# One-hot gates one tile later, and v rows ahead of u rows while the queries run

## The chip, the core and the metric

The kernel runs on one core of a Trainium2 chip. The metric is device time in microseconds (us) from start to end of one execution; the median of several executions is compared. The core has five engines with their own instruction streams: TensorE (PE, matmuls, with its weight loads shown as PEld), VectorE (DVE), ScalarE (ACT), GpSimd (POOL) and SyncE (SP). Here POOL issues the indirect gathers and SP issues nearly all other transfers.

## The reference, cut to what matters

One layer of a decoder: a state-space branch and a dilated attention branch are merged, and then each of 1,088 tokens goes through a retrieval layer (PEER) with 16,384 single-neuron experts. The change lies in this last layer. For a block of tokens it computes:

```
q = xb @ w_qp                                   # 8 heads, 2 halves of 128
s = q . sub_keys                                # 8 x 2 x 128 scores per token
sv, si = top_k(s, 16)                           # per head and half
cand = sv[0][:, None] + sv[1][None, :]          # 256 sums per head
best, pos = top_k(cand, 16); eidx = cidx[pos]   # 128 experts per token
gate = softmax(best)
act = gelu(xb . u_tab[eidx])                    # 128 dot products per token
out = (gate * act) . v_tab[eidx]                # 128 weighted rows per token
```

## The kernel before

The tokens are worked in two halves. The **first half** (512 tokens, four tiles of 128) gathers the rows of its chosen experts. The **second half** (512 tokens and 64 sample tokens, five tiles, the last of 64) computes all 16,384 experts densely. The gathers of the first half run beside the second half's work.

**The gather** (`gather`) is a Python generator that emits one row at a time. A *u row* (`gather_u`, L1558) is one indirect DMA on POOL of 128 expert rows of 1,024 floats (one per token) into one of eight `row` buffers (`RB`), followed by a multiply with row sum on DVE (L1562, "dot"). A *v row* of tiles 0 and 1 (`gather_v`, L1624) brings the 128 experts of one token; four of them make a batch that PE sums on column strips (L1640), with one small copy on DVE (L1635). The v rows of tiles 2 and 3 (`gather_w`, L1590) are added on DVE (L1596) and wait for the dense stage. So each tile has 128 u rows and 128 v rows. Which comes next is decided by

```python
pick = int(made[0] - made[1] >= LEAD)   # LEAD = 160; 1 is a v row
if not can[pick]:
    pick = 1 - pick
```

so that v rows start once u rows are 160 ahead and the two then take turns. How many rows are emitted is set by `tick(us)`: the surrounding code calls it with an estimate of its own time, and each row uses up 1.9 of it, times a rate that `pace` sets for the stage. `after` pins each row's instructions behind the last matmul (or, in `choose`, the last reduction) emitted before them. The dots and strip matmuls are emitted some rows later than their DMA (`late`, `catch_up`).

**The second half's routing** is `peer_keys(1)`, in this order: the norm of five tiles; the *queries*, 16 columns `c`, each a product with `w_qp` (L80, copied out by ACT at L1266), the scores against 128 keys (into a `tr` bank of PSUM, of which there are two) and `top16` of five tiles on DVE (L1304 to L1308, 25 instructions a column); then for each tile `choose` (DVE only: candidate sums L1330, eight `top16`, and 16 instructions that find the expert numbers, L1353 and L1354) and `gates`. `gates` turns a tile's choices into the dense gate matrix: DVE makes one-hots of the expert's row and column number for four tokens at a time (L1392, tile `oij`), ACT scales one by the gate (L1395, four instructions), PE multiplies them, ACT copies the result (L1397) into `Gt`, and after 32 tokens (a *block*; 18 blocks in all) `Gt` goes to DRAM (`G_scr`).

Between these steps `early` computes a block of 128 dense scores ahead (48 matmuls into `tr`, gelu on ACT at L1408, the weight split on ACT at L134 and DVE at L136): six times in each `choose`, once after each block of `gates`, twice in the queries; 50 in all. Then the dense stage begins, and its first weights read a piece of every block of `G_scr`.

The order of instructions on an engine is not wholly the order of the code: a list scheduler takes, at each free moment of an engine in its own estimate of time, the earliest instruction in code order that is ready. On the chip each engine then works through its list in that fixed order.

Of the kernel before, what the change touches and what calls it, by code (L numbers as in the profile page):

```python
# [36 lines left out]
FILL = (1.1, 2.274, 0.0, 0.8, 1.5, 0.05)  # L37
RATES = (1.0, 1.3, 1.0, 1.0, 0.86, 1.0, 0.6)
RB = 8
GL = 20  # L40
GO = (2, 0, 0.7)
LEAD = 160

VT = (2, 3)
SSMT = (10.0, 0.0, 5.0)
# [22 lines left out]
class Prog:  # L68
    def __init__(self, tc, a, stop=None):
        self.tc, self.nc, self.a, self.stop = tc, tc.nc, a, stop  # L70
        self.marks = []
        self.sides, self.inside, self.last, self.dn = {}, False, None, None

    def mark(self, name):
        n = [i.name for i in self.nc.cur_bb.bb.instructions[-1:]]
# [7 lines left out]

        self.sides[name] = [gen, rate, 0.0]

    def pace(self, name, rate):
        if name in self.sides:
            self.sides[name][1] = rate

    def tick(self, us):  # L90
        if self.inside:
            return
        for name in list(self.sides):
            s = self.sides[name]
            s[2] += us * s[1]
            while s[2] > 0 and name in self.sides:
                c = self.step(name)
                if name == "ahead":
                    us += c
# [1132 lines left out]
    def peer_keys(self, h):  # L1232
        tc, nc, a = self.tc, self.nc, self.a
        v = nc.vector
        nt = NT[h]
        ntl = len(TILES[NT[h]])
        es2 = ExitStack()
        self.pace(*(("gather", RATES[6]) if h else ("ahead", FILL[1])))
        x, (xp, g, x2) = self.xf, self.x2sb
        with ExitStack() as es:  # L1240
            esj = ExitStack()
            jk = esj.enter_context(tc.tile_pool(name=f"jk{h}", bufs=1, side="left" if h else "right"))
            for i in range(ntl):
                rows = 128 if i < 4 else 64
                r0 = h * 512 + i * 128 if i < 4 else 1024
                xn = jk.tile([128, D], F32, name="xn", tag="xn", bufs=2 + h)[128 - rows:]
                self.rms(xp, x2[i][128 - rows:], g[128 - rows:], xn, xn)
                if h == 0:
                    nc.sync.dma_start(self.xn2[r0:r0 + rows], xn)
                self.to_t(xn, rows, x, i * 128, 128 - rows)  # L1250
                self.tick(4.0)
            esj.close()
            self.esx2.close()
            if h:
                da = es.enter_context(tc.tile_pool(name="da", bufs=1))
            with tc.tile_pool(name=f"pk{h}", bufs=1, side="right") as kp, ExitStack() as eg:
                self.pace(*(("gather", RATES[2]) if h else ("ahead", FILL[2])))
                sv = [kp.tile([128, 16, 16], F32, name=f"sv{i}") for i in range(ntl)]
                si = [kp.tile([128, 16, 16], U32, name=f"si{i}") for i in range(ntl)]
                kq = eg.enter_context(tc.tile_pool(name=f"kq{h}", bufs=1, side="right"))  # L1260
                for c in range(16):
                    qp = kq.tile([128, nt], F32, name="qp", tag="qp", bufs=2)
                    keys = kq.tile([128, 128], F32, name="keys", tag="keys", bufs=3)
                    nc.sync.dma_start(keys, a["keys"][:, c])
                    for ps, (c0, c1) in zip(self.gemm_f(a["w_qp"][c], x, SPLITS[NT[h]]), SPLITS[NT[h]]):
                        nc.scalar.copy(qp[:, c0:c1], ps[:, :c1 - c0])  # L1266
                    pvs = []
                    for i in range(ntl):
                        rows = 128 if i < 4 else 64
                        if i % 4 == 0:  # L1270
                            ps = self.trt()
                        pvs.append(ps[:rows, (i % 4) * 128:(i % 4) * 128 + 128])
                        self.mm(pvs[i], qp[:, i * 128:i * 128 + rows], keys, start=True, stop=True)
                    for i in range(ntl):
                        rows = 128 if i < 4 else 64
                        rest = kq.tile([128, 128], F32, name="rest", tag="rest", bufs=3)[:rows]
                        self.top16(sv[i][:rows, c], si[i][:rows, c], pvs[i], rest)
                    self.tick(6.0)
                    if h and c in CE:
                        self.early(da, x)  # L1280
                self.pace(*(("gather", RATES[3]) if h else ("ahead", FILL[3])))
                eg.close()
                if h:
                    kg = eg.enter_context(tc.tile_pool(name="kg", bufs=1, side="right"))
                for i in range(ntl):
                    rows = 128 if i < 4 else 64
                    self.choose(kp, h, i, rows, sv[i], si[i], (lambda: self.early(da, x)) if h else None)
                    if h == 0:
                        self.tick(30.0)
                    if h == 0 and i == GO[0]:  # L1290
                        self.beside("gather", self.gather(), GO[1])
                    if h:
                        self.gates(kg, i, rows, lambda: self.early(da, x))
            if h:
                self.mark("dense")
                self.pace("gather", RATES[4])
                dn = self.dn = es2.enter_context(tc.tile_pool(name="dn", bufs=1, side="right"))
                self.dense(dn, da, x)
                es2.close()
        self.espx.close()  # L1300
# [205 lines left out]
    def gather(self):  # L1506
        nc, gp = self.nc, self.gp

        self.strips = gp.tile([128, NS, 2, 63], F32, name="strips")
        nc.gpsimd.memset(self.strips, 0.0)  # L1510
        yield RATE
        self.gw, self.ei = {}, {}

        self.late, self.wait = [], {}
        us, ws = [self.gather_u(i) for i in range(4)], [(self.gather_w if i in VT else self.gather_v)(i) for i in range(4)]

        nu = nv = 0
        made = [0, 0]
        while nv < 4:
            can = [nu < 4 and nu < nv + 3, nv < nu and (nv not in VT or self.dn is not None)]  # L1520
            if not any(can):
                yield RATE
                continue
            pick = int(made[0] - made[1] >= LEAD)
            if not can[pick]:
                pick = 1 - pick
            made[pick] += 1
            if next((us[nu] if pick == 0 else ws[nv]), None) is None:
                nu, nv = nu + 1 - pick, nv + pick
            else:  # L1530
                self.catch_up(2)
                yield RATE
        while self.late:
            self.late.pop(0)[1]()
# [210 lines left out]
```

## Time and profile before

| | |
|---|---|
| median of 3 runs | 4047.9 us (4040.63 to 4048.96) |
| profiled execution | 4032.86 us |
| its span, first to last instruction | 4031.1 us |
| busy share of PE, PEld, DVE, ACT, POOL | 93%, 84%, 73%, 36%, 36% |
| mean granted TensorE clock | 0.961 |

The busy time of an engine is the time in which at least one of its instructions runs; a share of it over the whole span mixes stages with different limits, so the stages have to be read one by one. The granted clock is 1 at 2.4 GHz and 0.5 at 1.2 GHz.

### The profile page before, as it was taken

The numbers are of one execution on the slowest core, as the hardware profiler recorded it, in microseconds if no ns is written. First come the engines' busy times: TensorE is split into PE (matmuls) and PEld (weight loads), VectorE is DVE, ScalarE is ACT, GpSimd is POOL, SyncE is SP. The second block draws the span as 40 slices with busy tenths as digits, with TensorE's granted clock in tenths as the row PEclk, the third lists the DMA queues.
The fourth block names the chain that finished last, engine by engine and source line by source line (L and its number), as shares of the span: only waits on it lengthen the run. The fifth ranks groups of instructions, "written<-read, shape, count | busy, mean of one in ns | idle before, by whom it ended". The sixth has DMA issues, their size and how long they took to land.

```text
span 4031.1 us, 72558 instructions
## 1 busy us (share of the span) xinstructions
PE 3738.5 (93%) x27907; PEld 3380.1 (84%) x27907; DVE 2943.4 (73%) x6796; ACT 1433.1 (36%) x2756; POOL 1444.1 (36%) x1236
## 2 busy tenths in 40 slices
PE   8889989899989967799979999879999999999997
PEld 8789965589878755597859899769999999999997
DVE  8627233445985767866999977668767999889986
ACT  3232224323234316322216888812222222222222
POOL 1620000000004424445563544433346755545550
PEclk9999989899999978899989999989999999999999
DMA  5574579544369989799897899999989999988993
GB/s 166 158 236 154 194 252 343 181 131 163 99 200 318 321 299 306 264 345 346 300 322 262 294 345 337 339 344 332 329 307 338 362 336 331 323 308 306 324 316 111
DMA packets 448987, 1112.83 MB, mean 276 GB/s; under 512 B 44656, under 2 KB 189424, under 8 KB 443008
## 3 DMA queue, kind: packets, MB, share of 16 engines
q1 hardware_dynamic: 301184, 571.26, 41.8%
q0 software_dynamic: 147456, 536.94, 37.0%
q8 instruction: 219, 3.59, 0.4%
q14 instruction: 128, 1.05, 0.1%
HBM read 991.77 MB, written 124.27 MB: 277 GB/s over the span
## 4 chain that ended last, share of the span: by engine, by line
PE 54%; DVE 6%; DMA 6%; issue 2%; ACT 2%; POOL 0%; SPq 0%; DVEq 0%; ACTq 0%; POOLq 0%
PE mm L80 31%; PE tr L80 20%; PE va L1640 2%; DVE row L1562 2%; DMA row<-in_u_tab,ei 1%; DMA G_scr<-Gt 1%; DMA Q<-Q_scr 1%; DVE wL L136 1%; DMA row<-in_v_tab,eT 1%; DMA V<-v_scr 0%; ACT Gt L1397 0%; DMA kT<-k_scr 0%; ACT sm L936 0%; DVE rest L1306 0%; DMA hs_scr<-Y 0%
## 5 line engine op out<-in xcount | busy, mean ns | idle before, releaser
L1558 POOL DMA_INDIRECT row<-in_u_tab,ei x512 | 664.3, 1297 | 986.7 <-DVE row L1562 451.3
L134 ACT CAST wH<-wraw 128x1024 fp32r<-128x1024 f32 (+1 forms) x476 | 492.3, 1035 | 1245.5 <-PE mm L80 915.5
L136 DVE TENSOR_TENSOR wL<-wraw,wH 128x1024 fp32r<-128x1024 f32 (+1 forms) x476 | 577.7, 1214 | 377.7 <-ACT wH L134 365.0
L1562 DVE SCALAR_TENSOR_TENSOR row<-row,gxn 128x1024 f32<-128x1024 f32 x512 | 616.8, 1217 | 48.4 <-DMA row<-in_u_tab,ei 41.8
L80 PE MATMUL tr<-x2H,wH 128*128 128x288 f32 x2048 | 611.7, 299 | 6.4 <-ACT a L1408 4.6
L80 PE MATMUL tr<-x2L,wH 128*128 128x288 f32 x2048 | 609.3, 297 | 0.0
L80 PE MATMUL tr<-x2H,wL 128*128 128x288 f32 x2048 | 609.1, 297 | 0.0
L80 PE MATMUL mm<-WH,wH 128*128 128x288 f32 (+2 forms) x2048 | 474.0, 295 | 18.6 <-ACT WH L186 18.2
L80 PE MATMUL mm<-WL,wH 128*128 128x288 f32 (+2 forms) x2048 | 473.8, 295 | 0.4 <-DVE WL L187 0.4
L80 PE MATMUL mm<-WH,wL 128*128 128x288 f32 (+2 forms) x2048 | 468.1, 294 | 0.0
L1590 POOL DMA_INDIRECT row<-in_v_tab,ei x256 | 350.9, 1371 | 293.3 <-DVE x3v L1596 240.7
L1624 POOL DMA_INDIRECT row<-in_v_tab,eT x256 | 315.7, 1233 | 386.4 <-DVE row L1562 228.4
L80 PEld LDWEIGHTS tr<-x2H,wH 128*128 128x128 f32 x2048 | 385.1, 188 | 16.3 <-ACT a L1408 7.2
L80 PEld LDWEIGHTS tr<-x2L,wH 128*128 128x128 f32 x2048 | 385.1, 188 | 2.5 <-issue 2.5
L80 PEld LDWEIGHTS tr<-x2H,wL 128*128 128x128 f32 x2048 | 385.0, 188 | 2.5 <-issue 2.5
L80 PEld LDWEIGHTS mm<-WH,wH 128*128 128x128 f32 x2048 | 339.8, 188 | 27.3 <-ACT WH L186 19.9
L80 PEld LDWEIGHTS mm<-WL,wH 128*128 128x128 f32 x2048 | 342.0, 188 | 4.1 <-issue 2.5
L80 PEld LDWEIGHTS mm<-WH,wL 128*128 128x128 f32 x2048 | 339.1, 188 | 1.7 <-issue 1.7
L1596 DVE SCALAR_TENSOR_TENSOR x3v<-row,act,x3v 128x1024 f32<-128x1024 f32 x256 | 327.4, 1279 | 3.0 <-DMA x3v<-x_scr 0.7
L80 PE MATMUL mm<-xnH,wL 128*128 128x288 f32 (+1 forms) x960 | 319.9, 333 | 2.7 <-DVE wL L136 2.7
L80 PE MATMUL mm<-xnH,wH 128*128 128x288 f32 (+1 forms) x960 | 322.3, 336 | 0.0
L80 PE MATMUL mm<-xnL,wH 128*128 128x288 f32 (+1 forms) x960 | 319.2, 332 | 0.0
(392 smaller groups left out, 7760.8 us busy)
## 6 DMA issues: line engine op xcount, KB each, us to landing
wraw<-in_vT SPq DMA_DIRECT2D x132, 512.0 KB
wraw<-in_uT SPq DMA_DIRECT2D x128, 512.0 KB
G_scr<-Gt SPq DMA_DIRECT2D x18, 2048.0 KB
G<-G_scr SPq DMA_DIRECT2D x32, 1152.0 KB
cc<-in_kc SPq DMA_DIRECT2D x48, 512.0 KB
cc<-in_vc SPq DMA_DIRECT2D x48, 512.0 KB
wraw<-in_w_g SPq DMA_DIRECT2D x32, 512.0 KB
wraw<-in_w_qp SPq DMA_DIRECT2D x32, 512.0 KB
```

What stands on the lines that cost most here:

```text
L80: self.last = self.nc.tensor.matmul(out, lhsT=lhsT, rhs=rhs, **kw)
L134: nc.scalar.copy(h, raw)
L136: nc.vector.tensor_sub(l, raw, h.bitcast(F32))
L1558: self.after(nc.gpsimd.indirect_dma_start(out=row, out_offset=None, in_=a["u_tab"], in_offset=bass.IndirectOffsetOnAxis(ap=ei[:, k:k + 1], ...
L1562: self.after(v.scalar_tensor_tensor(row, row, 1.0, xn, op0=ALU.mult, op1=ALU.mult, accum_out=act[:, k:k + 1]))
L1590: self.after(nc.gpsimd.indirect_dma_start(out=row, out_offset=None, in_=a["v_tab"], in_offset=bass.IndirectOffsetOnAxis(ap=ei[:, k:k + 1], ...
L1596: self.after(v.scalar_tensor_tensor(x3, row, self.gw[i][:, k:k + 1], x3, op0=ALU.mult, op1=ALU.add))
L1624: self.after(nc.gpsimd.indirect_dma_start(out=row, out_offset=None, in_=a["v_tab"], in_offset=bass.IndirectOffsetOnAxis(ap=eT[:, tk:tk + 1 ...
L1640: self.after(nc.tensor.matmul(va[0][c:c + 32, :], lhsT=self.strips[:, s, j, 31 - t - s:63 - t - s], rhs=rows[s * 2 + j][:, b * 512:(b + 1) ...
```

## The change

Two things are changed. In the second half's routing, the gates of a tile are emitted after `choose` of the next tile; those of the last tile come at the end. And in the norm and the queries of the second half the gather prefers v rows (`want`), with the condition that the u rows of the tile are all emitted and 12 rows more (`LATE`); while that does not hold, it emits u rows. After the queries `want` is empty again and the old rule holds.

```diff
+LATE = 12
...
-    def pace(self, name, rate):
+    def pace(self, name, rate, want=None):
         if name in self.sides:
             self.sides[name][1] = rate
+            if name == "gather":
+                self.want = want
...
-        self.pace(*(("gather", RATES[6]) if h else ("ahead", FILL[1])))
+        self.pace(*(("gather", RATES[6], "v") if h else ("ahead", FILL[1])))
...
-                self.pace(*(("gather", RATES[2]) if h else ("ahead", FILL[2])))
+                self.pace(*(("gather", RATES[2], "v") if h else ("ahead", FILL[2])))
...
-                    if h:
-                        self.gates(kg, i, rows, lambda: self.early(da, x))
+
+                    if h and i:
+                        self.gates(kg, i - 1, 128, lambda: self.early(da, x))
+                if h:
+                    self.gates(kg, ntl - 1, 64, lambda: self.early(da, x))
...
-            pick = int(made[0] - made[1] >= LEAD)
+            if nu < 4 and self.want == "v":
+
+                can[1] = can[1] and (not can[0] or made[0] >= 128 * nv + 128 + LATE)
+            pick = int(made[0] - made[1] >= LEAD) if self.want is None else int(self.want == "v")
             if not can[pick]:
                 pick = 1 - pick
```

## Rows read from the trace of the kernel before

**Rows 1.** The page: head line and busy line of its first part.
```profile
span 4031.1 us, 72558 instructions
...
PE 3738.5 (93%) x27907; PEld 3380.1 (84%) x27907; DVE 2943.4 (73%) x6796; ACT 1433.1 (36%) x2756; POOL 1444.1 (36%) x1236
```

**Rows 2.** Windows by stage: stretch, its length, busy us (instructions) per engine, clock.
```profile
1906.00:2000.00 94.00, 92.90 (x701) 82.25 (x700) 82.72 (x351) 22.00 (x38) 53.92 (x43) 1.00 0.90 303
2000.00:2104.00 104.00, 77.69 (x480) 56.47 (x480) 95.76 (x442) 12.50 (x21) 66.43 (x54) 0.82 0.89 318
2104.00:2157.00 53.00, 49.97 (x377) 44.59 (x376) 52.53 (x246) 18.59 (x29) 29.77 (x22) 1.00 0.92 327
2157.00:2340.00 183.00, 179.87 (x1399) 169.75 (x1398) 173.27 (x460) 149.40 (x321) 73.36 (x44) 0.98 0.79 270
2340.00:2580.00 240.00, 238.30 (x1893) 221.49 (x1893) 169.58 (x215) 205.74 (x461) 108.39 (x82) 1.00 0.98 341
2580.00:2660.00 80.00, 37.03 (x192) 25.53 (x192) 39.51 (x52) 37.83 (x86) 26.10 (x24) 0.71 0.94 339
2660.00:3985.00 1325.00, 1325.00 (x10017) 1294.54 (x10016) 1126.14 (x1639) 354.13 (x495) 657.02 (x497) 1.00 0.89 318
```

**Rows 3.** Windows of 10 us, the last stretch of the queries.
```profile
2090.00:2100.00 10.00, 5.81 (x26) 2.67 (x26) 9.27 (x46) 0.00 (x0) 5.32 (x5) 0.53 0.96 372
```

**Rows 4.** Waits between 1900 and 2120: who waited for whom, us, times, longest.
```profile
ACT qp L1266 <- PE tr L80: 59.7, 12, 9.9
...
ACT act L1568 <- DVE row L1562: 26.0, 1, 26.0
PEld tr L80 <- DVE rest L1306: 25.7, 8, 6.7
```

**Rows 5.** Windows of L1558 alone, the u rows issued by POOL.
```profile
1200.00:1920.00 720.00, 255.36 (x204) 0.92 0.89 313
1920.00:2105.00 185.00, 58.34 (x45) 0.90 0.90 313
2105.00:2624.00 519.00, 110.51 (x80) 0.98 0.90 314
```

**Rows 6.** Windows of L1624 alone, the strip v rows issued by POOL.
```profile
1200.00:1920.00 720.00, 59.48 (x54) 0.92 0.89 313
1920.00:2105.00 185.00, 55.25 (x46) 0.90 0.90 313
2105.00:2624.00 519.00, 115.31 (x80) 0.98 0.90 314
```

**Rows 7.** Windows of L1562 alone, the dots on DVE (two records each).
```profile
1920.00:2105.00 185.00, 54.67 (x90) 0.90 0.90 313
```

**Rows 8.** Chain that ended last: one batch of strips, and the end of the gates.
```profile
1851.33 1.85 PE va L1640 x16
...
2621.16 28.14 DMA G_scr<-Gt
...
2649.49 5.05 DMA G<-G_scr
```

**Rows 9.** Instruction groups by line: busy us, mean ns of one, idle before.
```profile
L134 ACT CAST wH<-wraw 128x1024 fp32r<-128x1024 f32 (+1 forms) x476 | 492.3, 1035 | 1245.5 <-PE mm L80 915.5 <-PE tr L80 187.0 <-issue 97.5
...
L1395 ACT ACTIVATE oij<-oij,T 128x128 f32<-128x128 f32 x576 | 180.2, 393 | 7.3 <-DVE oij L1392 6.9
...
L80 PE MATMUL mm<-oij 128*128 128x128 f32 x1152 | 172.1, 283 | 13.3 <-ACT oij L1395 13.3
...
L1397 ACT COPY Gt<-mm 128x512 f32<-128x512 f32 x144 | 155.1, 1107 | 57.0 <-PE mm L80 56.2
...
L1408 ACT ACTIVATE a<-tr 128x288 f32<-128x288 f32 x256 | 105.3, 412 | 241.2 <-PE tr L80 238.8 <-DVE row L1562 2.4
```

**Rows 10.** Timeline of DVE around the first one-hot.
```profile
2139.97 0.99 DVE L1304 MAX8 best<-look 128x8 f32<-128x50 f32 x8
...
2156.85 1.23 DVE L1392 TENSOR_TENSOR oij<-i,T 128x1024 f32<-128x1024 f32 x1
```

**Rows 11.** Windows of L1640 alone, the strip matmuls (PE, weight loads).
```profile
2105.00:2624.00 519.00, 43.42 (x320) 8.88 (x320) 0.98 0.90 314
2660.00:3985.00 1325.00, 36.56 (x304) 7.93 (x304) 1.00 0.89 318
```

More of the change, by code (lines that the diff above doesn't have):

```diff
@@ L71, in __init__ @@
         self.marks = []
-        self.sides, self.inside, self.last, self.dn = {}, False, None, None
+        self.sides, self.inside, self.last, self.dn, self.want = {}, False, None, None, None
     def mark(self, name):
```

## The prediction

> **What bounds the kernel now.** I read the page first. PE is busy for 93% of the 4031.1 us span [rows 1], and that share hides where it is not. So the second view is the windows by stage [rows 2]. In the dense stage, 2660 to 3985, PE is busy for all of 1325 us at full clock: every PE us that goes there costs one. In the queries, from 2000 to 2104, PE has 77.69 of 104 us and DVE 95.76: DVE sets the pace. From 2104 to 2340 both are nearly full (PE 229.8 and DVE 225.8 of 236, added from two rows). From 2340 to 2580 PE is full (238.30 of 240) and DVE has 70 us free. From 2580 to 2660 PE is busy for 37.03 of 80 us: the early score blocks have run out, and at the end a 28.14 us store of `Gt` and a 5.05 us load of `G` stand alone on the chain [rows 8].
>
> The third view is the waits of the queries [rows 4]. ACT waits 59.7 us for query matmuls, and PE's weight loads wait 25.7 us for `top16` (L1306), which frees the PSUM bank that the next scores need: the lag of DVE reaches PE. By 2090 to 2100 PE is busy for 5.81 of 10 us and the granted clock is 0.53 [rows 3], mostly the lower level of 1.2 GHz, after PE had stood still in pieces.
>
> The fourth view is the rows themselves. By 1920 POOL has issued 204 u rows and 54 strip v rows; in the queries 45 and 46; between 2105 and 2624 80 and 80 [rows 5, 6].
>
> **The change part by part.** *v rows first.* In the queries 91 rows are emitted, and `tick` does not change that. v rows are now taken until tile 0 has its 128: 128 - 54 = 74. Tile 1 may only start at 128 + 128 + 12 = 268 u rows, which is not reached, so the other 17 are u rows. 28 dots leave the queries and 28 v rows, seven batches, enter. A dot costs DVE 54.67 / 45 = 1.215 us [rows 7], together 34 us; a batch costs PE 1.85 us [rows 8], together 13 us.
>
> That is not a gain of 34 us. PE is full from 1906 to 2000 (92.90 of 94 us [rows 2]), and there the seven batches lengthen it, while DVE gets time that it can't use. The columns without dots cost DVE (82.72 + 95.76 - 54.67) / 16 = 7.7 us each, and the last three columns carry all 17 dots: 3 x 7.7 + 17 x 1.215 = 44 us. The first 13 go at PE's pace. PE did about ten columns in the 94 us, some 9.4 us each with five batches; without them 8.5, with 74 / 16 batches' worth of rows (1.4 a column, 2.6 us) 11.1 us. 1906 + 13 x 11.1 + 44 = 2094, against 2104 now: **-10 us**. Bounds: 0, if PE stands still for rows that have not landed (a batch now needs four of the eight buffers and nothing else runs between); -26, if all the idle time of PE from 2000 to 2104 goes. I take -10, which the two paces give.
>
> *The same rows later.* At the end of the queries there are now 221 u and 128 v rows, 93 apart, so the old rule first emits 67 u rows and then alternates. In the 160 rows up to 2624 that is 114 u and 46 v rows: sums of 335 and 174, where there were 329 and 180. The dense stage therefore finds about what it found, and its 36.56 us of strips [rows 11] stay. Between 2105 and 2624 PE loses 34 v rows, more than eight batches; I count the seven that went into the queries, 13 us, in a stretch where PE is busy for 97% or more until 2580: **-13 us**. Bounds: 0 and -16. DVE gets 28 to 34 dots, 34 to 41 us, and first into a stretch where it is full. What hides them is the 70 us that DVE has free from 2340 to 2580 [rows 2], as `choose` is needed only when its gates' turn comes. Without that cover they would cost 34 us.
>
> On this term a rule of the Trainium skill speaks against the sum: the page "Perfetto Trace Analysis", section "Identifying the Most-Contended Engine", says that matmul busy time is no good measure of how full TensorE is and that the share of weight loading is to be read beside it. That share is 221.49 of 240 from 2340 to 2580. By the rule PE had up to 18 us of room there and the 13 us might be nothing; by the matmul row they count. The sum goes by the matmul row, and the other case is a rival below.
>
> *Gates one tile later.* No instruction is added or removed; the six early blocks of each `choose` keep their place in it. In the code the second tile's `choose` now stands before the first gates. But the scheduler already had it there: its `top16` starts at 2139.97, before the first one-hot at 2156.85 [rows 10]. So at the start the move is worth nothing by itself. At the end it is not neutral. Gates of tile 3 and 4, six blocks, now stand behind all of `choose` with six early blocks among them, where there were twelve. A block costs ACT 8 x (180.2 + 155.1) / 144 = 18.6 us and an early block 1.035 + 2 x 0.412 = 1.9 us, 20.5 together [rows 9]. PE needs 8 x 172.1 / 144 = 9.6 us for the block, 48 x 1325 / 10017 = 6.3 us for the early one [rows 2, 9], and about 43.42 / 18 = 2.4 us of strips [rows 11]: 18.3. ACT becomes the slower one, by 2.2 us a block, 13 us over six. Bounds: 0 (the last blocks before had none left either) and +13; between them I take **+8 us**, nearer the upper, since early blocks that are used up sooner leave more of the end bare.
>
> Nothing new waits on SP or POOL: the same DMAs are issued, and only POOL's order of u and v rows changes. What is late next is the DVE work of `choose`, and the ACT list behind the gelu of tile 1's dots, which stood for 26.0 us [rows 4]: that gelu now falls among the gates.
>
> Sum: -10 - 13 + 8 = -15 us. The profiled execution took 4032.86 us, so 4017.9; the median of the runs is 1.0037 times it, so **4033 us**.
>
> **Rivals.**
> *The whole lag goes* (chance 0.12). PE's idle 26 us before 2104 vanish with the dots, and the clock stays up. -26 - 13 + 8 = -31: 4017. For it: the waits on `top16`. Against it: the 17 dots and the next 67 come at once after.
>
> *The strips were not on the path* (0.16). From 2340 to 2580 the work is held by ACT (205.74 of 240) and the weight loads as much as by matmuls; then the 13 us are not earned: -10 + 8 = -2: 4046. The page named above would read it so.
>
> *Only moved* (0.14). DVE is full from 2000 to 2340 and gets the same dots by its end; the 10 us won in the queries are lost again in `choose`, and the 13 us go to an end as long as before plus the 8 us: -13 + 8 = -5: 4043.
>
> *Gates start late* (0.28, the slower side). Two `choose` with some 32 u rows before the first gates, where DVE took 10 dots from 2104 to 2157: 22 x 1.215 = 27 us later, less the 10 won. ACT is busy for 393 of the 503 us from 2157 to 2660 [rows 2] and PE can't let it catch up. 27 - 10 + 8 = +25: 4073. It decides if the scheduler keeps one-hots behind the second `choose`; against it stands how early it mixed them before [rows 10]. It turns slower once the first one-hot lies more than about 10 us later than 2157.
>
> **How the numbers follow.** My forecast has 0.30, the likeliest case; the rivals have 0.12, 0.16, 0.14 and 0.28. A measurement of this kernel can tell about 0.2%, 8 us. Faster by more: the forecast and the whole lag, 0.42. Within it: the strips and the moved case, 0.30. Slower: 0.28. The range reaches from a little below the best case to the worst, 4014 to 4072, and leaves out less than 0.2 at its ends; the forecast's own, by the bounds of its terms, is 4017 to 4046.
>
> **What would show it.** In the queries: about 74 rows of L1624 and 17 of L1558 between the first and the last column, DVE clearly less than full for the first 13 columns, and the last `top16` near 2094. After them: u rows alone for some 67 rows, DVE full to about 2370, strips near 30 us of PE up to the end of the gates. At the end: the last early block more than two gate blocks before the last one. The first one-hot shows the slower rival: near 2157 or before it I am right, 20 us after it I am wrong. The prediction is also wrong if the split of rows at the start of the dense stage differs by more than a few batches, or if PE waits for v rows by more than 10 us in the queries.

## The result, and the profile after

The changed kernel takes 4068.27 us (median of 5 runs, 4064.05 to 4080.39), the kernel before 4046.97 us (5 runs, 4040.63 to 4048.96). The ratio is 1.0061, 95% interval 1.0043 to 1.0078: slower by 25 us by the ratio (0.0061 x 4047; 21 by the medians), where 4033 us and a gain were forecast. The profiled execution took 4067.84 us.

The windows by stage of the kernel after, with the columns of [rows 2]; the cuts are near the last copy of the queries (2088), the end of the last `top16` (2125), the first one-hot (2211) and the last `Gt` copy (2660):

```profile
1920.00:2088.00 168.00, 163.70 (x1231) 127.10 (x1229) 115.43 (x624) 33.37 (x56) 82.83 (x80) 1.00 0.89 304
2088.00:2125.00 37.00, 8.06 (x38) 7.39 (x39) 35.17 (x140) 0.86 (x3) 29.62 (x19) 0.58 0.84 300
2125.00:2211.00 86.00, 84.70 (x638) 84.46 (x637) 84.26 (x277) 29.57 (x48) 50.07 (x36) 1.00 0.92 342
2211.00:2420.00 209.00, 202.60 (x1573) 195.81 (x1571) 197.52 (x507) 167.92 (x356) 81.40 (x51) 0.99 0.81 283
2420.00:2570.00 150.00, 142.73 (x1115) 131.46 (x1116) 109.74 (x131) 127.92 (x290) 61.87 (x49) 0.99 0.95 334
2570.00:2660.00 90.00, 62.59 (x373) 51.76 (x376) 62.35 (x69) 81.27 (x197) 33.61 (x27) 0.88 0.87 283
2660.00:2700.00 40.00, 14.36 (x74) 9.21 (x67) 17.15 (x28) 4.02 (x6) 13.32 (x15) 0.63 0.99 372
2700.00:4020.00 1320.00, 1319.27 (x9972) 1290.03 (x9971) 1114.75 (x1622) 353.30 (x493) 645.46 (x489) 1.00 0.88 315
```

The dense stage is as full as before. In the queries VectorE has the room that was forecast (115.43 of 168 us). The new thing is the second line: for 37 us PE is busy for 8.06, at a granted clock of 0.58, while VectorE is full (35.17). Windows of single lines show what is in that stretch: first the u rows (L1567), then the strip v rows (L1633), then the dots (L1571, two records each), the counterparts of [rows 5 to 7].

```profile
1920.00:2088.00 168.00, 9.99 (x8) 1.00 0.89 304
2088.00:2125.00 37.00, 29.62 (x19) 0.58 0.84 300
2125.00:2211.00 86.00, 50.07 (x36) 1.00 0.92 342
...
1920.00:2088.00 168.00, 72.84 (x72) 1.00 0.89 304
2088.00:2125.00 37.00, 0.00 (x0) 0.58 0.84 300
2125.00:2211.00 86.00, 0.00 (x0) 1.00 0.92 342
...
1920.00:2088.00 168.00, 3.68 (x6) 1.00 0.89 304
2088.00:2125.00 37.00, 20.49 (x34) 0.58 0.84 300
2125.00:2211.00 86.00, 42.07 (x69) 1.00 0.92 342
```

The split of rows is nearly the one forecast, but not its place: 72 v rows and 8 u rows up to the last query copy, then 19 u rows in 37 us and 36 in the next 86, with no v row between. The waits of the kernel after between 1900 and 2120 say why (compare [rows 4]):

```profile
POOL row L1633 <- PE va L1649: 54.9, 18, 7.1
ACT qp L1269 <- PE mm L81: 37.0, 11, 6.2
...
PE tr L81 <- DVE rest L1312: 18.6, 2, 18.0
...
DVE row L1571 <- DMA row<-in_u_tab,ei: 10.1, 2, 8.3
```

While only v rows are fetched, all eight row buffers come free through PE's strips, and POOL stands 54.9 us for them. In the kernel before, its waits for strips were, by the same view:

```profile
POOL row L1558 <- PE va L1640: 14.0, 9, 2.6
...
POOL row L1624 <- PE va L1640: 5.7, 5, 2.5
```

The u rows behind the v rows in POOL's list come late: the first is issued at 2071.9 us, after the query copies of 15 of the 16 columns. That the buffers are the reason is read from these waits; no run had more of them. Then PE stands 18.0 us at a stretch for a PSUM bank whose `top16` (L1312) is queued on VectorE. The timeline of VectorE in the kernel after shows what it is queued behind:

```profile
2081.50 1.22 DVE L1571 SCALAR_TENSOR_TENSOR row<-row,gxn 128x1024 f32<-128x1024 f32 x1 [8.30 <-DMA row<-in_u_tab,ei]
...
2094.46 0.28 DVE L1310 MAX8 sv<-tr 128x8 f32<-128x128 f32 x1
2094.67 1.20 DVE L1571 SCALAR_TENSOR_TENSOR row<-row,gxn 128x1024 f32<-128x1024 f32 x1
2095.80 0.08 DVE L1571 DVE_READ_ACCUMULATOR row<-row,gxn 128x1 f32 x1
2095.80 1.21 DVE L1571 SCALAR_TENSOR_TENSOR row<-row,gxn 128x1024 f32<-128x1024 f32 x1
...
2098.00 0.27 DVE L1312 MATCH_REPLACE8 rest<-sv,tr 128x128 f32<-128x128 f32 x1
2098.20 1.20 DVE L1571 SCALAR_TENSOR_TENSOR row<-row,gxn 128x1024 f32<-128x1024 f32 x1
```

The first dot waits 8.30 us for its row, with `top16` work behind it on the engine; from then on a dot of 1.2 us stands between every few `top16` instructions of 0.28 us.

**From the queries' end to the first one-hot.** This stretch was 89.5 us in the kernel before (2067.4 to 2156.9) and is 122.9 us after (2088.2 to 2211.1). The groups of VectorE in it, by line, of the kernel before:

```profile
L1562 DVE SCALAR_TENSOR_TENSOR row<-row,gxn 128x1024 f32<-128x1024 f32 x21 | 25.3, 1211 | 4.6 <-DMA row<-in_u_tab,ei 4.3 <-DMA gxn<-xn_scr 0.3
L136 DVE TENSOR_TENSOR wL<-wraw,wH 128x1024 fp32r<-128x1024 f32 x8 | 9.7, 1210 | 0.0
...
L1353 DVE TENSOR_TENSOR df<-look,posf 128x128 int32<-128x128 f32 (+3 forms) x11 | 6.1, 557 | 0.1
```

and of the kernel after:

```profile
L1571 DVE SCALAR_TENSOR_TENSOR row<-row,gxn 128x1024 f32<-128x1024 f32 x52 | 62.4, 1213 | 1.8 <-DMA row<-in_u_tab,ei 1.8
L139 DVE TENSOR_TENSOR wL<-wraw,wH 128x1024 fp32r<-128x1024 f32 x14 | 17.1, 1218 | 1.7 <-ACT wH L137 1.7
...
L1359 DVE TENSOR_TENSOR df<-look,posf 128x128 int32<-128x128 f32 (+3 forms) x8 | 5.1, 633 | 0.0
```

31 dots more are 37.1 us, six weight splits more 7.4 us. `choose` itself is not more: of its `df` instructions, the first step in finding the expert numbers and eight a tile, there are 11 before and 8 after.

**The end of the gates.** The copies into `Gt` that come after the last early gelu, by the timeline of that line, in the kernel before:

```profile
L1397 ACT COPY Gt<-mm x18: 1023/1046/1110, 2579.8 to 2620.1; 128x512 f32<-128x512 f32 x18
```

and after:

```profile
L1403 ACT COPY Gt<-mm x42: 986/1052/1106, 2566.7 to 2656.0; 128x512 f32<-128x512 f32 x42
```

Eight copies are a block of gates, and these blocks are bare: no early score block is left to run beside them. 2.25 bare blocks in 40.6 us have become 5.25 in 89.6 us.

**The sum of it** is in the idle time of PE. I count it from a point early in the second half's queries, 920 us after the first query copy of the first half, to 20 us after the first load of `G`. The row of this window of the kernel before:

```profile
1911.70:2669.50 757.80, 680.65 (x5064) 605.42 (x5063) 618.20 (x1770) 446.23 (x952) 355.45 (x267) 0.94 0.90 316
```

and of the kernel after:

```profile
1913.50:2700.00 786.50, 684.00 (x5071) 612.27 (x5072) 624.16 (x1778) 446.14 (x954) 355.72 (x276) 0.94 0.89 310
```

PE is busy for nearly the same (680.65 and 684.00 us) and idle for 77.1 and 102.5: 25.4 of the 28.7 us by which the window is longer. From the first load of `G` to the end of the span it is 1381.6 and 1386.1 us.

Three rows of each kernel show where PE is idle after the last query copy: up to the first one-hot, from there to the last early gelu, and in the bare end. Before:

```profile
2067.40:2156.90 89.50, 73.78 (x507) 58.39 (x508) 83.96 (x393) 22.00 (x35) 53.61 (x42) 0.89 0.91 324
2156.90:2579.50 422.60, 417.77 (x3286) 390.84 (x3286) 342.57 (x673) 354.64 (x779) 181.84 (x126) 0.99 0.89 310
2579.50:2620.10 40.60, 27.28 (x157) 21.93 (x159) 28.93 (x33) 34.63 (x83) 12.61 (x10) 0.87 0.97 346
```

and after:

```profile
2088.20:2211.10 122.90, 92.85 (x675) 91.95 (x676) 119.33 (x416) 30.23 (x50) 79.60 (x55) 0.88 0.90 330
2211.10:2566.40 355.30, 344.11 (x2682) 326.07 (x2680) 303.90 (x634) 292.24 (x636) 143.09 (x99) 1.00 0.87 303
2566.40:2656.00 89.60, 62.55 (x368) 52.50 (x368) 64.38 (x71) 83.82 (x205) 32.79 (x26) 0.87 0.87 283
```

The idle time grows by about 14 us in the first stretch and 14 in the bare end, with 6 between them. So the stretch with the 37 us that catch the eye holds less than half of the growth.

### The profile page after: what moved, and what is told of

The parts are those of the page before. It is cut to its first block, busy times and chain, and to the rows that moved or that the text cites. A ratio compares the mean times of both kernels' runs of the same rounds, so it can differ in the third digit from the quotient of the medians.

```text
span 4066.1 us, 72466 instructions
## 1 busy us (share of the span) xinstructions
PE 3745.3 (92%) x27907; PEld 3391.0 (83%) x27907; DVE 2944.5 (72%) x6796; ACT 1432.6 (35%) x2756; POOL 1432.8 (35%) x1236
## 4 chain that ended last, share of the span: by engine, by line
PE 53%; DVE 5%; DMA 4%; ACT 4%; issue 3%; POOL 1%; SPq 0%; another core or an unknown queue 0%; POOLq 0%; DVEq 0%; ACTq 0%
PE mm L81 31%; PE tr L81 19%; PE va L1649 2%; DVE row L1571 2%; ACT Gt L1403 1%; ACT oij L1401 1%; DMA row<-in_u_tab,ei 1%; DMA row<-in_v_tab,eT 1%; DMA Q<-Q_scr 1%; DMA G_scr<-Gt 1%; ACT sm L939 1%; DVE wL L139 0%; POOL row L1633 0%; ACT wH L137 0%; PE tr L957 0%
## 5 line engine op out<-in xcount | busy, mean ns | idle before, releaser
L1567 POOL DMA_INDIRECT row<-in_u_tab,ei x512 | 669.6, 1308 | 1057.0 <-DVE row L1571 556.6
L1571 DVE SCALAR_TENSOR_TENSOR row<-row,gxn 128x1024 f32<-128x1024 f32 x512 | 617.5, 1220 | 54.7 <-DMA row<-in_u_tab,ei 47.1
L1633 POOL DMA_INDIRECT row<-in_v_tab,eT x256 | 299.3, 1169 | 351.3 <-DVE row L1571 176.4
L81 PEld LDWEIGHTS mm<-WH,wH 128*128 128x128 f32 x2048 | 340.4, 188 | 25.1 <-ACT WH L189 15.9
```

Of the source, the lines that this page charges most:

```text
L81: self.last = self.nc.tensor.matmul(out, lhsT=lhsT, rhs=rhs, **kw)
L1567: self.after(nc.gpsimd.indirect_dma_start(out=row, out_offset=None, in_=a["u_tab"], in_offset=bass.IndirectOffsetOnAxis(ap=ei[:, k:k + 1], ...
L1571: self.after(v.scalar_tensor_tensor(row, row, 1.0, xn, op0=ALU.mult, op1=ALU.mult, accum_out=act[:, k:k + 1]))
L1633: self.after(nc.gpsimd.indirect_dma_start(out=row, out_offset=None, in_=a["v_tab"], in_offset=bass.IndirectOffsetOnAxis(ap=eT[:, tk:tk + 1 ...
```

## The experiments

Each ratio below is to the kernel before on the same chip; its medians there were 4040.87, 4039.25 and 4040.11 us. Prices in us below are the ratio less 1, times 4040. The other columns come from one profiled execution each: from the last query copy to the first one-hot, PE's idle time in the window just defined, and the bare stretch from the last early gelu to the start of the last `Gt` copy.

| kernel | median us | ratio (95%) | to one-hot | PE idle | bare end |
|---|---|---|---|---|---|
| before | | | 89.5 | 77.1 | 40.6 |
| the change | 4068.27 | 1.0061 (1.0043 to 1.0078) | 122.9 | 102.5 | 89.6 |
| gates later alone | 4072.05 | 1.0075 (1.0056 to 1.0094) | 136.8 | 94.6 | 73.7 |
| v first alone | 4075.05 | 1.0082 (1.0064 to 1.0099) | 92.9 | 103.6 | 53.9 |
| change, short dots | 4023.45 | 0.9959 (0.9947 to 0.9971) | 100.7 | 63.9 | 71.4 |
| before, short dots | 4003.52 | 0.9920 (0.9902 to 0.9937) | 82.1 | 56.4 | 24.6 |
| change, early blocks late | 4061.89 | 1.0060 (1.0041 to 1.0079) | 109.7 | 99.2 | 71.1 |
| two v rows, one u row | 4045.43 | 1.0022 (1.0010 to 1.0033) | 89.3 | 78.3 | 49.0 |
| first gates at once | 4054.15 | 1.0044 (1.0026 to 1.0061) | 94.7 | 89.2 | 73.6 |
| the same, early spread | 4046.37 | 1.0022 (1.0008 to 1.0037) | 91.0 | 84.0 | 28.7 |
| all mends | 4038.47 | 1.0001 (0.9988 to 1.0014) | 89.1 | 73.8 | 36.3 |
| before, early spread | 4040.12 | 1.0003 (0.9991 to 1.0014) | 89.9 | 80.9 | 25.1 |
| before, v rows in `choose` | 4033.67 | 0.9987 (0.9972 to 1.0002) | 91.8 | 74.2 | 22.2 |
| the same, more of them | 4058.14 | 1.0045 (1.0028 to 1.0062) | 96.8 | 77.1 | 23.5 |

### The two parts alone

Gates one tile later, the gather as before:

```diff
-                    if h:
-                        self.gates(kg, i, rows, lambda: self.early(da, x))
+                    if h and i:
+                        self.gates(kg, i - 1, 128, lambda: self.early(da, x))
+                if h:
+                    self.gates(kg, ntl - 1, 64, lambda: self.early(da, x))
```

> The move of the gates alone; rows are chosen as before. Theory R (rows): the loss comes from the v rows, which leave the u rows to heap up at the end of the queries (in the changed kernel PE is busy for 10 of the 40 us from 2080 to 2120, and some 20 dots follow each other on VectorE there). Then this kernel is within 8 us of before, with its first one-hot between 2150 and 2175. Theory G (gates): the loss comes from the order of the second choose before the first gates and from the early blocks that are missing among the last six blocks. Then this kernel is 15 to 25 us slower, with its first one-hot at 2190 or later.

The v preference, the gates as before:

```diff
-        self.pace(*(("gather", RATES[6]) if h else ("ahead", FILL[1])))
+        self.pace(*(("gather", RATES[6], "v") if h else ("ahead", FILL[1])))
...
-            pick = int(made[0] - made[1] >= LEAD)
+            pick = int(made[0] - made[1] >= LEAD) if self.want is None else int(self.want == "v")
```

> The preference for v rows alone; each tile's gates follow its own choose as before. Theory R: 15 to 30 us slower than before, the last query product at about 2088 instead of 2067 and PE idle for some 30 us after it. Theory G: within 8 us of before, since the dots that come late are hidden in the gates' time.

Each alone costs about as much as, or more than, both together: 30 and 33 us, where the change costs 25; the intervals leave open whether more. In the first, VectorE's groups between the last query copy and the first one-hot are:

```profile
L1564 DVE SCALAR_TENSOR_TENSOR row<-row,gxn 128x1024 f32<-128x1024 f32 x29 | 34.9, 1214 | 3.3 <-DMA row<-in_u_tab,ei 3.3
L136 DVE TENSOR_TENSOR wL<-wraw,wH 128x1024 fp32r<-128x1024 f32 x14 | 17.1, 1218 | 2.8 <-ACT wH L134 2.6
L1355 DVE TENSOR_TENSOR df<-look,posf 128x128 int32<-128x128 f32 (+3 forms) x22 | 13.1, 593 | 0.2
```

22 `df` are nearly three tiles' choices, where before there were 11: the one-hots stand behind choices that nobody needs yet. In the second that stretch is hardly longer, 92.9 us, but PE stands still; its window around the last columns:

```profile
2080.00:2120.00 40.00, 11.78 (x70) 10.55 (x69) 38.31 (x132) 4.54 (x8) 31.90 (x21) 0.61 0.85 290
```

Together they are not the sum, and the groups above show an exchange: with both parts the first one-hot has 52 dots ahead of it, but one tile's choice instead of three. That the one's lateness covers the other's is my reading of these rows; no run was made for it alone. Nor does the first one-hot alone set the price: with v rows first alone it comes 92.9 us after the last query copy, with both parts 122.9 us, and the time is no shorter for it.

### Dots made short

In the changed kernel the dots of u rows 210 to 289 read 8 of 1,024 columns, so that most of these 80 products is left out; then the same in the kernel before:

```diff
-            def dot(row=row, k=k):
-                self.after(v.scalar_tensor_tensor(row, row, 1.0, xn, op0=ALU.mult, op1=ALU.mult,
+            def dot(row=row, k=k, w=8 if 210 <= i * 128 + k < 290 else D):
+                self.after(v.scalar_tensor_tensor(row[:, :w], row[:, :w], 1.0, xn[:, :w], op0=ALU.mult, op1=ALU.mult,
```

> The changed kernel, but the 80 dots of u rows 210 to 289 (those that leave the queries and those of the first two choose and gates) are computed over 8 of the 1,024 columns; all transfers stay. This leaves out part of 80 dot products per token and takes about 80 x 1.1 = 88 us of VectorE out of the stretch from 2080 to 2270. Theory R, in the form that VectorE's dots are what delays choose: the first one-hot comes 30 to 50 us earlier than in the changed kernel (2211) and the kernel is 20 to 40 us faster than it, so as fast as before or faster. Theory R in the form that the landing of the rows delays PE and choose, not the dots: under 10 us faster than the changed kernel. Theory G: 10 us or less.

> The kernel before with the same 80 dots (u rows 210 to 289) over 8 of 1,024 columns; it leaves out that part of the sums, as the run with short dots of the changed kernel did. If VectorE's dots before the first gates are what the change adds (theory C), this kernel gains clearly less from it than the changed one's 45 us: 10 to 25 us, and the two with short dots lie within 20 us of each other. If the dots cost the same in both (theory E), it gains 40 us or more, and the change's own cost is elsewhere.

The changed kernel gains 41 us by it (1.0061 to 0.9959), with its first one-hot at 2190.5 us, 21 us earlier where 30 to 50 were expected. The kernel before gains 32 (to 0.9920), between the bounds of the control's two theories. With short dots the two lie 16 us apart, without them 25. So the dots of this stretch are on the path in both kernels, and only some 9 us of what the changed kernel gains can belong to the change; the intervals leave 0 to about 20 for it. The run of the changed kernel alone would have looked like proof of the whole.

### The u rows spread over the queries

The v preference alone, but after two v rows one u row:

```diff
-            pick = int(made[0] - made[1] >= LEAD) if self.want is None else int(self.want == "v")
+            pick = int(made[0] - made[1] >= LEAD) if self.want is None else int(sum(made) % 3 > 0)
```

> The v preference of the change alone, but in the queries two v rows are followed by one u row, so that the u rows do not all come at the end of the queries. If the heap of dots behind the last column is what costs (theory H), the last query copy is within 5 us of before, there is no stretch of 30 us with PE nearly idle, and the time is at most 12 us above before. If the moved dots themselves cost, wherever they lie (theory M: they fall into choose and the gates), it is 20 to 35 us above before as with the whole preference.

The ratio falls from 1.0082 to 1.0022. The last query copy comes earlier here (2072.6 us, where it was 2087.5), so the stretches from it to the first one-hot are compared, first with the full preference, then with two v rows to one u row:

```profile
2087.50:2180.40 92.90, 51.97 (x355) 51.10 (x356) 90.92 (x350) 16.22 (x27) 60.17 (x39) 0.75 0.85 314
...
2072.60:2161.90 89.30, 73.94 (x498) 62.62 (x499) 80.00 (x360) 19.22 (x31) 52.51 (x45) 0.86 0.92 335
```

PE is idle for 40.9 us in the one and 15.4 in the other, as in the kernel before (15.7). That speaks for the heap. But the mend does more than spread it: 27 u rows were issued from 1920 to 2088, where the full preference issued 9, so fewer dots were put off as well.

### The first gates at once, and the bare end

The gates' move without its first step, in the order choose 0, gates 0, choose 1, choose 2, gates 1 and so on:

```diff
+                    if h and i != 1:
+                        self.gates(kg, max(i - 1, 0), 128, lambda: self.early(da, x))
+                if h:
+                    self.gates(kg, ntl - 1, 64, lambda: self.early(da, x))
```

> The gates' move alone, but the first tile's gates stay right behind its own choose; tiles 1 to 4 come one tile later. Theory S (all of the move's price is the late first one-hot): within 8 us of before. Theory B (the order of the rest and the bare end cost too): 15 to 30 us slower than before.

The stretch to the first one-hot is back at 94.7 us and the price falls from 30 to 18 us, but is not gone. The bare end is 73.6 us, as with the whole move. Three runs tried that end. In the changed kernel five early blocks went from `choose` to the last gates:

```diff
-EQ = (0, 1, 3, 5)
+EQ = (0, 1, 3)
...
+            if i == 3 or (i == 4 and b == 0):
+                between()
```

> The changed kernel with five early blocks moved from the five choose (one from each) to the gates of the last tiles (two after each of five of the last six blocks); 50 in all as before. In the changed kernel the last early block lies near 2570 and 38 of 144 one-hots follow it, with PE busy for 62.6 of 90 us. If the bare end costs what PE's idle time there suggests (my term of 8 us, or up to the 27 us of idle time), this kernel is 8 to 25 us faster than the changed one; if ScalarE sets the pace of the end anyway, it is within 6 us of it.

In the kernel with the first gates at once, nine:

```diff
-            if between and q in EQ:
+            if between and q in (EQ[:1] if i > 1 else EQ):
...
         for b in range(R // 32):
+            for _ in range((i == 3) + (3 - b) * (i == 4)):
+                between()
```

> The gates' move with the first gates at once, and nine early score blocks moved from the choices of tiles 2 to 4 to before the last six blocks of gates. Without that the stretch from the last early gelu to the last Gt copy was 73.6 us, against 40.6 in the kernel before, and the time 15 us above before. Theory B (the bare end is the rest of the price): the bare stretch shrinks to 40 us or less and the time comes within 8 us of before. Theory O (the blocks are only missed elsewhere, PE has to stand still in the choices instead): bare stretch short, time still 10 us or more above before.

And in the kernel before six, from the choices of tiles 3 and 4 (`i > 2` above) to the last two blocks, three before each:

> The kernel before with six early blocks moved from the choices of tiles 3 and 4 to before the last two blocks of gates, whose 40.6 us had none. Theory B (a bare end costs): bare stretch below 25 us and 5 to 15 us faster than before. Theory O (missed elsewhere): within 5 us of before, or slower.

The nine blocks cut the bare end to a block and a half; the copies into `Gt` after the last early gelu of that kernel:

```profile
L1401 ACT COPY Gt<-mm x12: 1025/1050/1095, 2598.7 to 2626.2; 128x512 f32<-128x512 f32 x12
```

The ratio went from 1.0044 to 1.0022, but the intervals overlap. In the kernel before, 15 us less of bare end gave nothing (1.0003), and in the changed one 18 us less no difference that the intervals allow. A price of the bare end is therefore not shown: the ratios put 9 us on 45 us of it in the one kernel, with 0 to about 18 by the intervals, and at most 4 us on 15 us of it in the kernel before.

### All mends together

Two v rows to one u row, the first gates at once, and the nine early blocks moved:

> The whole change with three mends: in the queries two v rows to one u row, the first tile's gates right behind its own choice, and the nine early blocks moved as in the run above. If the heap of dots, the late first one-hot and the bare end are all of the price (theory A): within 8 us of before. If something of the two moves is left (theory L): 12 us or more above before.

It takes what the kernel before takes (1.0001), and PE's idle time is 73.8 us against 77.1. So the three places that the mends touch hold all of the price that can be measured, and nothing is won by what is left of the change. How much each mend gives back in the changed kernel itself is not shown, and the first two take back part of the change.

### v rows in the choices instead

If dots before the first gates cost, taking them out of `choose` and the gates of the kernel before should help. There the lead that u rows need was lowered from 160 to 110, and to 70, at the start of the choices:

```diff
+                if h:
+                    self.lead = 110
...
-            pick = int(made[0] - made[1] >= LEAD)
+            pick = int(made[0] - made[1] >= self.lead)
```

> The kernel before, but from the start of choose on v rows are preferred until u rows are only 110 ahead: some 25 dots go from choose and the first gates to the dense stage and v rows come in their place; queries and gates stay as before. Theory V (the dots that VectorE does ahead of the first one-hots set the time): 25 x 1.2 = 30 us of VectorE leave the stretch from 2100 to 2340, the first one-hot comes earlier by up to 15 us and the dense stage starts 8 to 20 us earlier, so 8 to 20 us faster than before. Theory P (PE is full there and pays for the strips what VectorE gains): within 8 us of before.

> The same with u rows only 70 ahead: some 45 dots leave choose and the gates and some 80 v rows come first. Theory V: more than in the run with 110, 15 to 30 us faster than before. Theory P: the strips and the wait for row buffers take it back: no faster than the run with 110, or slower.

With 110 it is not to be told from the kernel before (0.9987, to 1.0002); with 70 it is slower by 18 us. The idle time of PE before the dense stage is then that of the kernel before (77.1 us), but PE is busy for 700.95 us in the window, where it was 680.65: the v rows are paid in PE's time, as theory P said. The strips are only moved, though: in the window they take 100.37 us instead of 76.78, and behind it 11.55 instead of 36.56 [rows 11]. The dense stage should give the time back and does not: from the first load of `G` to the end of the span it is 1384.7 us, 3 us more than before. To it the dots were sent (252.56 us of VectorE behind the window, 208.06 before). Two windows of the kernel with 70, in a stretch where PE had been full before [rows 2]:

```profile
2700.00:2900.00 200.00, 194.18 (x1453) 183.66 (x1452) 163.72 (x301) 48.15 (x59) 94.37 (x63) 0.99 0.91 326
2900.00:3100.00 200.00, 188.80 (x1380) 187.63 (x1379) 185.76 (x271) 49.00 (x68) 113.64 (x84) 0.97 0.93 337
```

PE is idle there for 17 us that it was not idle for, and VectorE has 185.76 of 200 in the second. Theory V's gain did not come with 70; with 110 the point is 5 us, and the interval reaches to 11, so a small gain is not excluded.

## Why the prediction was wrong, point by point

**The queries, -10 us: wrong in sign.** The step that failed is the sum by two paces, 13 columns at PE's pace and then "the last three columns carry all 17 dots". The first pace was about right: PE did the columns at 163.70 of 168 us, with 38.48 us of strips from 1913.5 to 2088.2, where the kernel before had 18.80 from 1911.7 to 2067.4. (The "74 / 16" written there does not give its 1.4 batches a column; 74 rows over 13 columns, four to a batch, do.) But I put the u rows into the last columns by code order. They lie behind v rows in POOL's list, and those wait for buffers that PE's strips free (54.9 us). So 3 dots lie before the last query copy and 17 in the 37 us after it, in front of the last `top16`, and PE stands still in them. The last `top16` ends at 2126 us, where I had 2094; before it was 2108, not the 2104 that I counted from. I had named the wait for rows as the bound "0, if PE stands still for rows that have not landed", and kept it at 0; the price is beyond that bound, 33 us for the v preference alone.

**The strips out of the gates, -13 us: moved, not earned.** After the last query copy the strips up to the load of `G` take 30.59 us instead of 57.97, twice what I had counted (27 us). PE's idle time after that copy rose more, up to 20 us after the load from 63.5 to 96.8 us (77.1 and 102.5 less 13.6 and 5.7 before the copy). The cover that I named for the late dots, 70 us that VectorE had free from 2340 to 2580, lies too late: VectorE is full up to 2420 (197.52 of 209), and the one-hots wait in that line. So the strips that left earned nothing that the runs show; that VectorE's order is what held PE there is read from these rows. The rule of the Trainium skill that was weighed there ("Perfetto Trace Analysis", "Identifying the Most-Contended Engine"), which puts the share of weight loads in the place of matmul busy time, does not decide it: by matmuls or by weight loads, both readings price PE's work, and what grew was PE's waiting.

**Gates one tile later, 0 at the start: the second step that failed.** I argued that "the scheduler already had it there", as the second tile's `top16` began before the first one-hot [rows 10]. It had three `df` of the second tile there; with the move alone it put nearly three tiles' choices ahead. The move alone made the stretch up to the first one-hot 47 us longer and the kernel 30 us slower, and putting the first gates back took off 12 of that. In the changed kernel the step fails otherwise: only one tile's `df` are ahead of the first one-hot there, but 31 dots more. On top of v rows first alone (33 us) the move adds no price that shows.

**The bare end, +8 us:** the mechanism is there and larger than forecast (89.6 us instead of 40.6, with 27.1 us of idle PE instead of 13.3), the price is not shown by any of three runs.

**The rivals.** "Gates start late" (+25 us, 4073) is the case that came, with the sign by which I had said it decides: the first one-hot lies 54 us later. Its price is the one measured, its mechanism holds only in part, and that the number fits is partly luck. The scheduler did not keep the one-hots behind the whole second `choose` (8 `df` ahead of them). I had put 22 dots more ahead of the one-hots, and 31 more were there; but 19 of the 52 us (both counted from the first query copy of the first half) were there by the end of the queries, where I had thought 10 won. What I held against it, one early instruction taken as the order of a whole list, was weak evidence.

## What to carry to other kernels

When work is taken off one engine for a stretch, follow the buffers: when only the full engine frees them, everything behind them in the queue is held up, and what was put off arrives in one heap. An order in code is not an order on the engine: count whole groups of instructions ahead of the one in question, not one that starts early. Look for idle time between two fixed points of the program: the most striking gap lay in a stretch with less than half of the growth here. A run that makes a suspected cost small needs its control in the old kernel: here 32 of 41 us were gained there too.

## What the runs showed that was not expected

The parts' prices do not add: 30 and 33 us alone, 25 together. And the profiled executions differ before the change can act: the first query copy of the first half lies between 988.7 and 1004.3 us, and the stretch from it to the last query copy was 8.5 us longer with the early blocks of the last two tiles moved, an edit wholly behind it, than in the kernel before. Points of time of two executions were therefore compared over short stretches, and differences under 9 us between single profiles were not read.
